# Six buffers instead of four for the two parts of every weight tile, and a 512-byte descriptor region

## The chip, the core and the metric

The kernel runs on one core of a Trainium2 chip. The metric is the device time of one execution in microseconds, the median of three runs. The engines are named as in the profile: PE multiplies matrices (PEld is its loading of weights), DVE, ACT and POOL work element by element, and SP only issues DMA transfers. Each engine takes its instructions strictly in the order in which the program gives them.

## The reference

For 256 tokens of width 1024 the reference computes a first block of two layers (pooling, an attention over chosen keys, a memory attention, three gated branches), a second block (a gated delta rule run over the tokens from both ends, a short convolution, two gated branches), and a gated MLP. All of it is float32. What matters here is the second block and the shape that all products with weights share:

```python
# every projection, shortened
proj = h @ w            # h: 256 x 1024, w: 1024 x (multiples of 256), float32

# second block, shortened: per head, from both ends of the sequence
S_t = exp(g_t) * S_{t-1} + beta_t * k_t (v_t - k_t S_{t-1} exp(g_t))^T
o_t = q_t S_t
y   = gate_dn * (norm(o) * silu(z)) @ w_branch_dn + gate_sc * conv(...) @ w_branch_sc
out = x + y @ w_out
```

## The kernel before, in words

**A product with weights.** PE multiplies in a float32 format of reduced precision, so an operand is split in a high part H and a low part L = value − H, and a product is the sum of three: xH·wH, xL·wH and xH·wL. The activations (names xH and xL) are split once. A weight matrix comes in blocks of 256 columns; a block with 1024 rows is two tiles of 128 partitions x 4 x 256 (512 KB each). For each tile SP issues the load (load(), L92 to L95, name raw, five buffers), ACT writes the high part (L107, name wH, four buffers), and DVE subtracts (L110, name wL, four buffers); in stretches where pool_l is 3, every third of these subtractions is POOL's. A *unit* of work for PE is one block: 2 halves of 128 columns x 8 row tiles x 3 products = 48 matmuls (mm3(), L123, from unit() or unit2(); units() at L151 runs two blocks side by side, with a part of the rows first). Four buffers hold the tiles of two units, six those of three.

**The second block.** After the first block's last product, x is scaled and split (L186), its squares are summed (L622, L625), PE adds them over the partitions (L631, name st), ACT takes the root (name sd), and DVE the reciprocal (L635, name St). Every result of q, k, v, z, the gates and the convolution is multiplied by St (for instance L672), so it is the first thing that all of DVE's later work in the block needs. The small product for the two gates of the delta rule (name ba, 48 columns) stands around it.

**The side chain.** delta() (L835 to L963) is a generator. Between units, pump() runs it on by a few steps, so its instructions are strewn among the units of q, k, v, z, the convolution (w_sc, w_branch_sc) and the gates (w_gate). It makes decay matrices (E, L899), inverts 32x32 blocks on DVE (inverse_blocks(), tm at L828, Tb at L830), copies the result transposed (L943, name Lb), sends both through memory (L946, to sT), and reads them back in three layouts (load_inverse(), L998 Tn, L1000 TBX, L1003 TT), all of it on SP's queue, between the weight loads. meta_state() (L967 to L986) makes the state after 16 leading tokens (names mtp, mkv at L976, mvn at L979, a copy on ACT at L980, ms at L984). whole_inverse() begins with the matmuls named x at L1016, which need Tn and TBX. Then half() and norm_gate() run for the heads 0 to 3 and 4 to 7: ks (L1082, L1084), vn (L1088, L1089), the states, the outputs o (L1119, L1123, copied at L1125), squares (L1134, osq) and their sums (L1136, osum), the norm (L1143) and the gate.

**What follows the chain.** drain() (L1228) empties the generator; its result is split (L1236, L1237, name oHL) and goes into the product with w_branch_dn (units(), L151, name mml), whose first part needs the heads 0 to 3 alone. Then come w_out_2 and the MLP.

**What sets the order.** The program is written in the order of the text, but the order in which each engine takes its instructions is chosen by a scheduler (`schedule_with_timeline_sim=True`, L1426), which plays the program through on a modelled timeline and also knows when a buffer comes free. With other numbers of buffers it chooses another order for all engines.

```python
for b in (1, 2):
    nc.sync.dma_start(out=TBX[32 * b:32 * b + 32, :, 0:32], in_=sT[0, b, 2 - b].rearrange("u i j -> i u j"))
...
TT, Tn, TBX = load_inverse(sT)
...
Sf0 = [meta_state(hf, mTt, dm) for hf in range(2)]
yield 2.0
for cst in whole_inverse(TT, Tn, TBX, LT64, LT32, nb64, nb32):
    yield cst
```

Of the kernel before, what the change touches and what calls it, by code (L numbers as in the profile page):

```python
# [8 lines left out]
F32R = mybir.dt.float32r  # L9
# [42 lines left out]
class _K:  # L52
# [44 lines left out]
    def weights(self, blk, kt, n):  # L97

        nc = self.nc
        parts = {}  # L100
        k0 = 0
        while k0 < kt:
            raw = self.ahead.pop(0) if self.ahead else self.load(blk, k0, min(4, kt - k0), n)
            m = raw.shape[1]
            H = self.wp.tile([128, 4, n], F32R, tag="wH", name="wH", bufs=4)[:, :m, :]
            L = self.wp.tile([128, 4, n], F32R, tag="wL", name="wL", bufs=4)[:, :m, :]
            nc.scalar.activation(H, raw, AF.Copy)  # L107
            self.n_l += 1
            e = nc.gpsimd if self.pool_l and self.n_l % self.pool_l == 0 else nc.vector
            e.tensor_tensor(L, raw, H.bitcast(F32), op=OP.subtract)  # L110
            for i in range(m):
                parts[k0 + i] = H, L, i
            k0 += m
        return [lambda k, a=a: parts[k][a][:, parts[k][2], :] for a in range(2)]
# [59 lines left out]
    def hl(self, pool, src, shape, tag, bufs=1):  # L174
        nc = self.nc
        H = pool.tile(shape, F32R, tag=tag + "H", name=tag + "H", bufs=bufs)
        L = pool.tile(shape, F32R, tag=tag + "L", name=tag + "L", bufs=bufs)
        nc.scalar.activation(H, src, AF.Copy)
        nc.vector.tensor_tensor(L, src, H.bitcast(F32), op=OP.subtract)
        return H, L  # L180

    def scaled_hl(self, H, L, x, g):

        nc = self.nc
        nc.scalar.activation(H, x, AF.Copy, scale=g)
        nc.vector.scalar_tensor_tensor(L, x, g, H.bitcast(F32), op0=OP.mult, op1=OP.subtract)  # L186
# [1244 lines left out]
```

## Time and profile before

| | |
|---|---|
| median of three runs | 1180.29 us (1178.58 to 1182.12) |
| profiled execution, its own time | 1179.4 us |
| its span | 1177.4 us |
| PE busy | 1114.1 us (95%), 9536 matmuls |
| DVE busy | 869.0 us (74%) |
| ACT busy | 586.7 us (50%) |
| POOL busy | 383.5 us (33%) |

The times that stand in front of a row count from the start of the span; the execution's own time is 2.0 us longer than the span. A busy time says how long an engine worked, not how long others waited for it. The views are read by stages: the first block (until about 570 us), the second block with its side chain (570 to 990), the MLP (990 to the end).

### The profile page before, as it was taken

The numbers are of one execution on the slowest core, as the hardware profiler recorded it, in microseconds if no ns is written. First come the engines' busy times: TensorE is split into PE (matmuls) and PEld (weight loads), VectorE is DVE, ScalarE is ACT, GpSimd is POOL, SyncE is SP. The second block draws the span as 40 slices with busy tenths as digits, with TensorE's granted clock in tenths as the row PEclk, the third lists the DMA queues.
The fourth block names the chain that finished last, engine by engine and source line by source line (L and its number), as shares of the span: only waits on it lengthen the run. The fifth ranks groups of instructions, "written<-read, shape, count | busy, mean of one in ns | idle before, by whom it ended". The sixth has DMA issues, their size and how long they took to land.

```text
span 1177.4 us, 23260 instructions
## 1 busy us (share of the span) xinstructions
PE 1114.1 (95%) x9536; PEld 1086.1 (92%) x9536; DVE 869.0 (74%) x1220; ACT 586.7 (50%) x883; POOL 383.5 (33%) x304
## 2 busy tenths in 40 slices
PE   6999999999999999999999878698899999999996
PEld 6999999999999999999998878697799999999996
DVE  8668897678665897977899899996547497555543
ACT  6344546446344454455675947242235645444442
POOL 8102310003100040100854668933011157534353
PEclk9999999999999999999999979898899999999999
DMA  7765453565655544455544525454432355556561
GB/s 262 268 211 170 156 173 123 180 192 182 196 192 182 179 133 136 147 177 180 186 169 144 181 82 144 134 175 105 148 126 94 134 187 180 200 172 199 180 193 40
DMA packets 68514, 194.63 MB, mean 165 GB/s; under 512 B 19504, under 2 KB 21816, under 8 KB 67896
## 3 DMA queue, kind: packets, MB, share of 16 engines
q1 hardware_dynamic: 66056, 188.72, 49.9%
q10 hardware_dynamic: 2352, 4.43, 1.1%
q8 instruction: 74, 1.21, 0.4%
q14 instruction: 32, 0.26, 0.1%
HBM read 189.39 MB, written 5.30 MB: 165 GB/s over the span
## 4 chain that ended last, share of the span: by engine, by line
PE 70%; DVE 17%; DMA 4%; issue 3%; ACT 2%; POOL 2%; SPq 1%; DVEq 0%; ACTq 0%; POOLq 0%
PE mm L123 49%; PE mml L151 8%; PE mmd L1302 5%; DVE wL L110 4%; DVE ac L685 2%; DVE Tb L830 1%; PE hp L372 1%; ACT wH L107 1%; DMA sT<-Lb 1%; DMA rows<-scr 1%; DVE tm L828 1%; DVE vf L685 1%; DVE kq L713 1%; PE mo L495 1%; PE vn L1088 1%
## 5 line engine op out<-in xcount | busy, mean ns | idle before, releaser
L110 DVE TENSOR_TENSOR wL<-raw,wH 128x1024 fp32r<-128x1024 f32 (+2 forms) x292 | 395.9, 1362 | 156.4 <-ACT wH L107 139.4
L107 ACT ACTIVATE wH<-raw 128x1024 fp32r<-128x1024 f32 (+3 forms) x347 | 347.0, 1034 | 302.4 <-PE mm L123 150.2
L123 PE MATMUL mm<-xH,wL 128*128 128x256 f32 (+3 forms) x1720 | 247.7, 284 | 11.2 <-DVE wL L110 11.2
L123 PE MATMUL mm<-xH,wH 128*128 128x256 f32 (+3 forms) x1720 | 249.0, 286 | 5.6 <-ACT ac L680 1.8
L123 PE MATMUL mm<-xL,wH 128*128 128x256 f32 (+3 forms) x1720 | 248.6, 285 | 0.0
L123 PEld LDWEIGHTS mm<-xH,wL 128*128 128x128 f32 (+1 forms) x1720 | 221.9, 190 | 13.5 <-DVE wL L110 12.3
L123 PEld LDWEIGHTS mm<-xH,wH 128*128 128x128 f32 (+1 forms) x1720 | 222.7, 190 | 9.5 <-ACT ac L680 2.0
L123 PEld LDWEIGHTS mm<-xL,wH 128*128 128x128 f32 (+1 forms) x1720 | 223.2, 191 | 2.8 <-issue 2.2
L110 POOL TENSOR_TENSOR wL<-raw,wH 128x1024 fp32r<-128x1024 f32 (+2 forms) x55 | 133.9, 2434 | 217.5 <-ACT wH L107 149.3
L397 POOL TENSOR_TENSOR bp<-bias,sc 128x1024 f32<-128x1024 f32 (+1 forms) x4 | 14.7, 3667 | 246.3 <-DVE sc L395 219.9
L123 PE MATMUL mm<-yH,wH 128*128 128x256 f32 x256 | 42.5, 286 | 4.9 <-ACT yH L1207 4.9
L123 PE MATMUL mm<-yL,wH 128*128 128x256 f32 x256 | 43.0, 286 | 4.3 <-DVE yL L1208 4.3
L123 PE MATMUL mm<-yH,wL 128*128 128x256 f32 x256 | 42.1, 285 | 0.0
L191 POOL TENSOR_TENSOR acc<-x 128x256 f32<-128x256 f32 x2 | 1.4, 722 | 123.6 <-DVE x L562 120.4
L123 PEld LDWEIGHTS mm<-yH,wH 128*128 128x128 f32 x256 | 35.6, 193 | 5.2 <-ACT yH L1207 5.1
L123 PEld LDWEIGHTS mm<-yL,wH 128*128 128x128 f32 x256 | 35.7, 193 | 5.1 <-DVE yL L1208 4.8
L123 PEld LDWEIGHTS mm<-yH,wL 128*128 128x128 f32 x256 | 35.5, 193 | 0.3 <-issue 0.3
L193 POOL TENSOR_TENSOR sq<-x 128x256 f32<-128x256 f32 x33 | 33.6, 1027 | 6.2 <-DVE x L562 5.5
L685 DVE SCALAR_TENSOR_TENSOR ac<-rc,cw,ac 128x271 f32<-128x271 f32 (+3 forms) x48 | 34.4, 753 | 0.0
L191 POOL TENSOR_TENSOR a<-x 128x256 f32<-128x256 f32 x3 | 2.8, 941 | 80.4 <-DVE x L562 74.8
L1302 PE MATMUL mmd<-aH,wH 128*128 128x256 f32 x176 | 28.6, 281 | 0.0
L1302 PE MATMUL mmd<-aH,wL 128*128 128x256 f32 x176 | 28.6, 281 | 0.0
(433 smaller groups left out, 1829.3 us busy)
## 6 DMA issues: line engine op xcount, KB each, us to landing
raw<-in_w_b SPq DMA_DIRECT2D x64, 512.0 KB, 4.1
raw<-in_w_a SPq DMA_DIRECT2D x55, 512.0 KB, 4.0
raw<-in_w_gu SPq DMA_DIRECT2D x44, 512.0 KB, 4.5
raw<-in_w_branch SPq DMA_DIRECT2D x24, 512.0 KB, 4.3
raw<-in_w_out SPq DMA_DIRECT2D x24, 512.0 KB, 3.8
raw<-in_w_qkv SPq DMA_DIRECT2D x24, 512.0 KB, 3.8
raw<-in_w_sc SPq DMA_DIRECT2D x24, 512.0 KB, 3.8
raw<-in_w_down SPq DMA_DIRECT2D x20, 512.0 KB, 4.4
```

Source lines behind the costliest of these rows:

```text
L107: nc.scalar.activation(H, raw, AF.Copy)
L110: e.tensor_tensor(L, raw, H.bitcast(F32), op=OP.subtract)
L123: self.last_mm = nc.tensor.matmul(ps, lt(a, kt), rt(b, kt), start=i == 0, stop=i == n - 1).ins
L151: self.last_mm = self.nc.tensor.matmul(ps[:, :N], w[a](k)[:, h * 128:h * 128 + 128], xs[b][:, k, :], start=k == 0 and (a, b) == (0, 0), st ...
L193: nc.gpsimd.tensor_tensor(tmp, x, x, op=OP.mult)
L372: nc.tensor.matmul(pp[p][:, j, :n], a[r, 2 * i + j, :], b(r, 2 * i + j), start=True, stop=True)
L397: nc.gpsimd.tensor_tensor(bp[:, :, :n], bias[:, :, off:], pen[:, None, :n].to_broadcast([128, 8, n]), op=OP.add)
L495: nc.tensor.matmul(ps[:, h, :], mv[:, mb, h * 128:h * 128 + 128], PT[:, mb, h, :], start=mb == 0, stop=mb == 1)
L685: V.scalar_tensor_tensor(ac[:, t0:t1], r[:, t0 + j - 2:t1 + j - 2], w[:, j:j + 1], ac[:, t0:t1], op0=OP.mult, op1=OP.add)
L713: (V if (i * 8 + h) % 3 else G).tensor_tensor(t, t, sl(h, i), op=OP.mult)
L828: eng.tensor_tensor(t, Lb[:, j + 1:, j:j + 1].to_broadcast([P, m, w]), Tb[:, j:j + 1, 0:w].to_broadcast([P, m, w]), op=OP.mult)
L1302: nc.tensor.matmul(pss[h][:, :S], w[a](k)[:, h * 128:h * 128 + 128], (aH, aL)[b][:, k0 + k, :], start=k0 + k == 0 and (a, b) == (0, 0), st ...
```

## The change

The two tile calls in weights() ask for six buffers instead of four. One buffer is 4 x 256 x 4 = 4096 bytes in each of the 128 partitions, so the four new ones take 16 KB of each partition. The call that makes the program sets the region that is kept in each partition for descriptors of transfers issued by software to 512 bytes, where it had 16384.

```diff
@@ -102,8 +102,8 @@
-            H = self.wp.tile([128, 4, n], F32R, tag="wH", name="wH", bufs=4)[:, :m, :]
-            L = self.wp.tile([128, 4, n], F32R, tag="wL", name="wL", bufs=4)[:, :m, :]
+            H = self.wp.tile([128, 4, n], F32R, tag="wH", name="wH", bufs=6)[:, :m, :]
+            L = self.wp.tile([128, 4, n], F32R, tag="wL", name="wL", bufs=6)[:, :m, :]
@@ -1419,7 +1419,7 @@
-    nc = bacc.Bacc("TRN2", target_bir_lowering=False, num_devices=1)
+    nc = bacc.Bacc("TRN2", target_bir_lowering=False, num_devices=1, dynamic_dma_scratch_size=512)
```

The counts of instructions stay as they are; the order on each engine moves. Three places are shown. The first is DVE at the start of the second block, around the reciprocal St. The number behind a name tells one tile of that name from another: wL_7093 is the second tile of the small product ba, wL_7336 belongs to the third unit after it. Before:

```order
L625 SCALAR_TENSOR_TENSOR a2_6848<-a1_6847,a2_6848 128x256
L110 TENSOR_TENSOR wL_7093<-raw_7090,wH_7092 128x192
L110 TENSOR_TENSOR wL_7166<-raw_7163,wH_7165 128x1024
L635 RECIPROCAL St_6845<-sd_7039 128x272
L672 TENSOR_TENSOR rc_7048<-mml_6937,St_6845 128x272
```

And now, from the same sum of squares to the same first use of St:

```order
L625 SCALAR_TENSOR_TENSOR a2_6848<-a1_6847,a2_6848 128x256
L110 TENSOR_TENSOR wL_7248<-raw_7245,wH_7247 128x1024
L110 TENSOR_TENSOR wL_7254<-raw_7251,wH_7253 128x1024
L110 TENSOR_TENSOR wL_7336<-raw_7333,wH_7335 128x1024
L635 RECIPROCAL St_6845<-sd_7039 128x272
L672 TENSOR_TENSOR rc_7048<-mml_6937,St_6845 128x272
```

Three subtractions stand where two stood, and they are those of later tiles; wL_7336 is the sixth tile behind wL_7093 and is written into the same buffer. On PE the last matmuls that read wL_7093 stand behind the sum st (name st2 here) from which St is made:

```order
L123 MATMUL mm2_7096<-xH_6811,wL_7087 48x272 x3
L631 MATMUL st2_7037<-a2_6848,ones_79 128x272
L201 MATMUL stat_7043<-a1_6847,ones_79 128x256
L123 MATMUL mm2_7096<-xH_6811,wL_7087 48x272
L123 MATMUL mm2_7096<-xH_6811,wL_7093 48x272 x4
```

So 19 of the 24 matmuls of ba now stand ahead of the sum, where all 24 stood behind it, and wL_7336 cannot be written before the last 4 have been done.

The second place is SP's queue around the transfers of the inverse through memory (sT). Before:

```order
L94 DMA raw<-in_w_sc 128x1024 x11
L94 DMA raw<-in_w_gate 128x1024 x2
L94 DMA raw<-in_w_branch_sc 128x1024
L946 DMA sT<-Tb 4x16x1024 x2
L946 DMA sT<-Lb 4x16x1024 x2
L998 DMA Tn<-sT 32x16x32 x2
L1000 DMA TBX<-sT 32x16x32
L998 DMA Tn<-sT 32x16x32 x2
L1000 DMA TBX<-sT 32x16x32
L1003 DMA TT<-sT 32x32x32 x4
L94 DMA raw<-in_w_gate 128x1024 x2
L94 DMA raw<-in_w_branch_sc 128x1024
```

Now:

```order
L94 DMA raw<-in_w_gate 128x1024 x2
L94 DMA raw<-in_w_branch_sc 128x1024
L94 DMA raw<-in_w_gate 128x1024 x2
L94 DMA raw<-in_w_branch_sc 128x1024
L94 DMA raw<-in_w_gate 128x1024
L946 DMA sT<-Tb 4x16x1024 x2
L946 DMA sT<-Lb 4x16x1024 x2
L998 DMA Tn<-sT 32x16x32 x2
L1000 DMA TBX<-sT 32x16x32
L94 DMA raw<-in_w_gate 128x1024
L998 DMA Tn<-sT 32x16x32 x2
L1000 DMA TBX<-sT 32x16x32
```

Four weight loads that stood behind the whole passage through sT stand ahead of it, and a fifth in its middle.

The third place is PE at the end of the side chain, from the last ks of the heads 4 to 7 on. Before:

```order
L1082 MATMUL ks<-Sfb,kq 128x128 x3
L123 MATMUL mm<-xL,wH 128x256 x2
L123 MATMUL mm<-xH,wL 128x256 x8
L123 MATMUL mm<-xH,wH 128x256 x8
L123 MATMUL mm<-xL,wH 128x256 x6
L1088 MATMUL vn<-vb,TT 128x128 x2
L1119 MATMUL o<-kq,Sf_9375 128x128
```

Now, to the first matmuls of w_branch_dn (mml):

```order
L1082 MATMUL ks<-Sfb,kq 128x128 x2
L1088 MATMUL vn<-vb,TT 128x128
L1119 MATMUL o<-kq,Sf_9375 128x128
...
L1123 MATMUL o<-At,vb 128x128 x2
L1136 MATMUL osum<-osq,ones 128x512
L151 MATMUL mml<-oHL,wH 128x256 x20
L1136 MATMUL osum<-osq,ones 128x512
L151 MATMUL mml<-oHL,wH 128x256 x10
L151 MATMUL mml<-oHL,wL 128x256 x4
```

The matmuls of the last gate units, 82 of which stood between this ks and the product with w_branch_dn, now stand ahead of the ks; none is left behind it.

## Rows read from the trace of the kernel before

**Rows 1.** The page: busy time of each engine with its share and its count, and the clock that PE was granted, one digit (tenths of full speed, 9 is 90% or more) for each fortieth of the span.

```profile
PE 1114.1 (95%) x9536; PEld 1086.1 (92%) x9536; DVE 869.0 (74%) x1220; ACT 586.7 (50%) x883; POOL 383.5 (33%) x304
...
PEclk9999999999999999999999979898899999999999
```

**Rows 2.** Busy time of each engine in stretches of the span. The columns are the stretch, its length, the busy time (and instructions) of PE, PEld, DVE, ACT and POOL, PE's granted clock, the share of the DMA engines and GB/s.

```profile
60.00:475.00 415.00, 414.60 (x3522) 404.94 (x3523) 312.64 (x469) 203.20 (x310) 53.17 (x51) 1.00 0.54 171
475.00:515.00 40.00, 38.46 (x339) 37.46 (x340) 34.18 (x48) 20.06 (x37) 4.67 (x1) 1.00 0.45 146
570.00:804.30 234.30, 202.60 (x1521) 195.12 (x1519) 221.55 (x331) 139.01 (x240) 150.33 (x128) 0.94 0.48 152
804.30:831.70 27.40, 19.70 (x130) 17.76 (x131) 12.37 (x20) 7.19 (x11) 4.52 (x4) 0.80 0.57 153
831.70:931.60 99.90, 99.59 (x1202) 96.75 (x1202) 56.51 (x91) 42.13 (x54) 13.38 (x6) 0.97 0.32 106
...
1020.00:1050.00 30.00, 30.00 (x257) 30.00 (x256) 16.55 (x16) 13.53 (x16) 13.09 (x7) 1.00 0.56 180
```

**Rows 3.** Waits over the whole span, by the waiting engine and line and the engine and line that ended the wait: us in total, how often, the longest.

```profile
ACT wH L107 <- PE mm L123: 150.2, 68, 5.2
...
PE mm L123 <- DVE wL L110: 11.2, 6, 5.6
...
PE mvn L979 <- DVE mkv L976: 4.7, 1, 4.7
```

**Rows 4.** The timeline around St. The columns, here and in the timelines below, are start, duration (of the whole group where a count stands at the end), engine, line, operation and shapes; in brackets the engine's idle time before it and what ended it.

```profile
583.79 0.70 PE L631 MATMUL st<-a,ones 128*128 128x272 f32 x2 [0.40 <-PE mml L151]
...
584.57 1.33 PE L123 MATMUL mm<-xH,wH 128*48 128x272 f32 x8
...
585.20 1.85 DVE L635 RECIPROCAL St<-sd 128x272 f32<-128x272 f32 x1 [0.36 <-ACT sd L89]
...
586.74 1.16 PE L123 MATMUL mm<-xH,wL 128*48 128x272 f32 x8
...
588.49 1.22 DVE L110 TENSOR_TENSOR wL<-raw,wH 128x1024 fp32r<-128x1024 f32 x1
```

**Rows 5.** The timeline from the end of the block inverse on DVE to the first matmul of whole_inverse().

```profile
804.27 1.03 DVE L943 COPY Lb<-Tb 128x1024 f32<-128x1024 f32 x1
...
807.55 0.41 DVE L1188 TENSOR_TENSOR cS<-mm,St 128x258 f32<-128x258 f32 x1
...
819.27 0.48 SPq L1000 DMA_DIRECT2D TBX<-sT  x1
...
823.22 0.98 SPq L94 DMA_DIRECT2D raw<-in_w_gate  x2
...
828.08 1.06 ACT L107 ACTIVATE wH<-raw 128x1024 fp32r<-128x1024 f32 x1 [8.01 <-DMA raw<-in_w_gate]
829.04 0.57 ACT L980 ACTIVATE mkv<-mvn 16x512 f32<-16x512 f32 x1
...
829.67 2.07 PE L984 MATMUL ms<-mkv 16*128 16x128 f32 x8 [5.46 <-ACT mkv L980]
...
831.67 0.26 PE L1016 MATMUL x<-Tn,LT 32*32 32x32 f32 x1
```

**Rows 6.** Transfers issued between 790 and 835 us: count, KB each, median us from issue to landing.

```profile
TBX<-sT SPq DMA_DIRECT2D x2, 64.0 KB, 7.1
```

**Rows 7.** The timeline at the end of the side chain.

```profile
913.32 1.13 DVE L1084 SCALAR_TENSOR_TENSOR vb<-ks,be,vb 128x128 f32<-128x128 f32 x4 [0.60 <-PE ks L1082]
...
923.59 0.61 PE L1123 MATMUL o<-At,vb 128*128 128x128 f32 x4
...
928.66 1.02 PE L1136 MATMUL osum<-osq,ones 128*128 128x512 f32 x2
...
930.42 1.06 ACT L107 ACTIVATE wH<-raw 128x1024 fp32r<-128x1024 f32 x1
...
937.23 1.13 ACT L1236 ACTIVATE oHL<-vf 128x512 fp32r<-128x512 f32 x2
```

**Rows 8.** The timeline of DVE and POOL at one place of the block inverse, and all 31 instructions of DVE's line there (ns: least, median and longest; the first and the last start; the most frequent shapes).

```profile
749.93 5.05 DVE L830 TENSOR_TENSOR Tb<-Tb,tm 128x112 f32<-128x112 f32 x1
...
750.22 2.33 POOL L110 TENSOR_TENSOR wL<-raw,wH 128x1024 fp32r<-128x1024 f32 x1
...
752.52 2.33 POOL L929 TENSOR_TENSOR qb<-kq,Gb 128x1024 f32<-128x1024 f32 x1
...
L830 DVE TENSOR_TENSOR Tb<-Tb,tm x31: 193/390/5054, 743.8 to 804.0; 128x31 f32<-128x31 f32 x2, 128x60 f32<-128x60 f32 x2, 128x87 f32<-128x87 f32 x2, 128x112 f32<-128x112 f32 x2
```

**Rows 9.** The timeline of PE near the end of the first block.

```profile
495.36 0.74 PE L123 MATMUL mm<-xH,wL 128*128 128x256 f32 x4 [0.73 <-DVE wL L110]
...
502.21 0.74 PE L123 MATMUL mm<-xH,wH 128*128 128x256 f32 x4 [0.81 <-ACT wH L107]
```

**Rows 10.** The page: the DMA queues with their kind, packets, MB and share of the 16 engines' span.

```profile
q1 hardware_dynamic: 66056, 188.72, 49.9%
q10 hardware_dynamic: 2352, 4.43, 1.1%
q8 instruction: 74, 1.21, 0.4%
q14 instruction: 32, 0.26, 0.1%
```

## The prediction

> **What bounds the kernel now.** First the page's busy times: PE 95%, DVE 74%, ACT 50% [rows 1]; the reader sees one engine that is nearly always busy, so deeper buffers can win at most what PE still waits. Then the windows, to see where PE is not busy [rows 2]. From 60 to 475 us PE works 414.60 of 415.00 us, and nothing that DVE or ACT do earlier can help. From 570 to 804.3 PE works 202.60 of 234.30, and DVE 221.55: this stage belongs to DVE (12.75 us idle). From 804.3 to 831.7 neither is full (19.70 and 12.37 of 27.40): a stage of waits. From 831.7 to 931.6 PE is full again (99.59 of 99.90). Then the waits [rows 3]: ACT waits 150.2 us in 68 places for PE to free a buffer of wH, while PE waits for DVE's wL only 11.2 us, in 6 places. So most of the time the four buffers are full because PE is the slow one; more buffers let DVE and ACT run further ahead, which pays only where PE later finds work that it had to wait for. The longest single wait of PE that hangs on this is in [rows 5]: ms at 829.67 waited 5.46 us for a copy on ACT, and that copy stood behind a wH conversion that waited 8.01 us for its weight load.
>
> **The change part by part.** Instruction counts stay, so all of it is order and waits. The sum is made against the profiled execution (1179.4, span 1177.4), 0.9 us under the median of 1180.29.
>
> *St.* St starts at 585.20 [rows 4]. In the new order the third subtraction ahead of it, wL_7336, goes into the buffer of wL_7093, which PE frees with ba's last 4 matmuls. A matmul of ba takes 1.16/8 = 0.145 us [rows 4]. Without the old order PE would start ba at 583.79 − 0.40 = 583.39; 19 matmuls take it to 586.15, st and stat some 0.7 more (by the same row), 5 matmuls 0.7: free at 587.5. On DVE the subtraction (1.22 us [rows 4]) then ends at 588.7, and St starts 3.3 us later than before (588.5; I take a little off because POOL may do a share of DVE's earlier work). Behind the waiting subtraction on DVE stands St and so everything that needs St. Below zero it can't go, since three more subtractions of 1.22 us stand ahead of St than before; above, it is 3 × 1.22 = 3.7. So 0 to 3.7, taken 3.3, near the upper end, because DVE is the bound of this stage.
>
> *DVE from St to Lb.* 35 subtractions stand there before and after. Two more small operations fall into it, 0.41 us each [rows 5]: +0.8. POOL gets one more subtraction (2.33 us [rows 8]) ahead of Lb; POOL and DVE disturb each other (rival 2), for which I take half of it, +1.2, between 0 and 4.7 (two of them). Lb moves from 804.27 to 804.27 + 3.3 + 0.8 + 1.2 = 809.6.
>
> *From Lb to x (L1016).* Before, 831.67 − 804.27 = 27.4 us, of which the last part was ms, waiting for ACT, waiting for a load of w_gate that was issued at 823.22 only, since it stood behind the passage through sT on SP's in-order queue [rows 5]. Four of those loads stand ahead of the passage now, so this wait of 5.46 goes. What is late next is TBX: issued at 819.27, landing 7.1 us later [rows 5, 6], at 826.4, which is 22.1 us behind Lb. So x starts between 22.1 and 27.4 us behind Lb; the upper end is the case where the five loads of 512 KB moved in front take from the transfers what the wait gives back. I take 22.1, the chain that is left: 809.6 + 22.1 = 831.7, the same as before. The gain in this stage and the loss in front of it cancel.
>
> *Work pulled ahead of x.* By the new order 5788 matmuls of weights and of the chain stand ahead of the first x on PE where 5759 stood, 29 more. From x on PE is full, so they come off what follows: 29 × 30.00/257 = 29 × 0.117 [rows 2] = −3.4. If PE had to wait inside the stage for these as well, it is 0; if x moves, it moves with it.
>
> *The end of the chain.* Before, 82 matmuls of the gates stood between the last ks and the product with w_branch_dn and filled PE's waits; now nothing but the first part of w_branch_dn does (the 64 matmuls that read heads 0 to 3 alone). The chain from ks to the split result: 1.13 for the vb on DVE, about 7.1 for vn and o on PE (the o at 923.59 ends the work that in the new order is packed), 0.6 for the copy, 0.62 for the squares, and from osum to oHL 937.23 − 928.66 = 8.57 less the 1.06 of a wH conversion that stood in it [rows 7] = 7.5, then 0.6 to the end of the first half of oHL: 17.6 us. PE's work beside it is 7.1 of vn and o, 1.0 of osum [rows 7], 64 × 0.117 = 7.5: 15.6. What is left open is 2.0, so +2.0 (from 0, if the wH conversions in between move off the chain and the first 64 are slowed, to 3.2 with the conversion back in it). The 82 matmuls are not lost: they were done earlier, where PE would have had to do something else.
>
> *The first block.* Near its end PE waits 0.73 for wL and 0.81 for wH [rows 9], in a window with 1.54 us open [rows 2]. Deeper buffers should remove one of the two: −0.8 (0 to −1.5).
>
> *The region.* All queues are fed by hardware or by instructions [rows 10], none by software descriptors; a smaller region costs 0.
>
> Sum: 0 at x, −3.4, +2.0, −0.8 = −2.2. 1179.4 − 2.2 = 1177.2, and with the 0.9 between execution and median 1178.1.
>
> **The rivals.** *Rival 1, DVE has room: faster.* The 12.75 us that DVE idles between 570 and 804.3 [rows 2] take up the late St, the two operations and POOL's share, and Lb stays at 804.27; x then starts at 826.4, 5.3 us earlier: 1178.1 − 5.3 = 1172.8. For it: DVE's idle time is not one wait that is fixed. Against it: the idle time is spread, and the chain of the inverse on DVE has only short steps with nothing between. The furthest end of this case is that all waits of PE for wL go, 11.2 us [rows 3]: 1180.29 − 11.2 = 1169.1. The Trainium skill's "Perfetto Trace Analysis" (Identifying the Most-Contended Engine) says that the same gap repeating on the engine that should be saturated can mean that there is no room in SBUF or PSUM for the next tile. By that rule the added buffers should close the gaps, and the time would be at that end; the trace agrees only in part, since six waits make up the 11.2 us and ACT's 150.2 point the other way.
>
> *Rival 2, DVE and POOL collide more often: slower.* The place is the side chain on DVE between St and Lb. At 749.93 a Tb takes 5.05 us where the median of the line is 0.39; in the same time POOL runs two operations of 2.33 us [rows 8]. So one collision costs DVE 2.3 us (one POOL operation) to 4.7 (5.05 − 0.39). The new order puts other, and more, POOL subtractions beside DVE's. Three more such meetings of 2.33 make 7.0, and Lb and x move by as much: 1178.1 + 7.0 = 1185.1. It decides from about 5.7 us on (1183.8 − 1178.1), that is from three short or two long meetings. For it: this stage is DVE's, and POOL works 150.33 of 234.30 us in it [rows 2]. Against it: the number of POOL's operations hardly changes, and new meetings replace old ones. The Trainium skill's "SBUF — State Buffer" (SBUF: two separate sides) says that the shared port pair is an exclusive lock, held for a whole instruction by whichever of a DVE operation with two SBUF inputs and a POOL operation starts first. The trace agrees: 5.05 is two POOL operations of 2.33 and the 0.39.
>
> *Rival 3, nothing that counts moves.* The buffers are full because PE is slow (150.2 us of ACT's waits); the order of the side chain changes, but the sums of it cancel to zero: 1180.3.
>
> PE's clock is a cost that I put at nothing: it was granted 0.94, 0.80 and 0.97 of full speed in the three windows from 570 to 931.6 [rows 2], so it stood for part of them at the lower of its two levels (1.2 instead of 2.4 GHz). If the stage from 804.3 on ran at full clock, that is at most 27.4 × 0.20 = 5.5 us; if it fell as low in one more stretch of that length, as much is lost. This widens the range on both sides and is in both rivals' chances.
>
> **How the numbers follow.** Within 0.3% of 1180.29 (1176.7 to 1183.8) is about what a measurement of this kernel can't tell from no change. My forecast has a chance of 0.42, with its own range of 1174.5 to 1182 from the bounds of its terms; of that 0.10 lies under 1176.7, 0.30 inside and 0.02 above. Rival 1 has 0.24, all faster. Rival 2 has 0.22, all slower. Rival 3 has 0.12: 0.10 inside and 0.01 on each side. Together faster 0.35, same 0.40, slower 0.25. The range goes from 1169 (the furthest end of rival 1) to 1187 (rival 2 with about four meetings: 1178.1 + 9.3).
>
> **What would show it.** St should start near 588.5 instead of 585.20, in the row where DVE's wL before it waits for PE's mm; Lb near 809.6. The wait of ACT for in_w_gate (8.01) and that of PE at ms (5.46) should be gone, and PE should wait before x (L1016), released by the transfer to TBX or Tn. Behind the last ks PE should show waits of 2 us in all, at vn or at mml for oHL. Rival 1 would show Lb at 804 to 805; rival 2 rows of L828, L830 or L685 on DVE of 2 to 7 us beside POOL's subtractions, more of them than before. The prediction is wrong if PE gets waits in 60 to 475 us, if the window from 831.7 on is no longer full, or if the stage between Lb and x stays at 27 us with another load in the place of w_gate's.

## The result and the profile after

The changed kernel takes 1187.99 us (median of 4 runs, 1185.71 to 1189.34) against 1180.99 of the kernel before, run beside it (4 runs): a ratio of 1.0063, 95% interval 1.0042 to 1.0083. A second job gave 1187.87 and 1.0067 (1.0044 to 1.0091). It is slower by 7 us, clear of noise; 1178.1 was forecast, and the range ended at 1187.

The profiled execution took 1188.02 us, its span is 1186.2. The windows with the borders of [rows 2], and one for the first 75 us:

```profile
60.00:475.00 415.00, 412.28 (x3491) 403.14 (x3490) 311.23 (x465) 201.70 (x309) 53.00 (x51) 1.00 0.53 172
475.00:515.00 40.00, 39.21 (x352) 38.11 (x351) 36.96 (x52) 22.28 (x39) 4.67 (x1) 1.00 0.45 145
...
570.00:804.30 234.30, 206.00 (x1542) 199.33 (x1540) 217.45 (x317) 138.01 (x240) 153.18 (x130) 0.95 0.47 152
804.30:831.70 27.40, 23.21 (x168) 21.50 (x168) 22.41 (x42) 11.09 (x16) 10.78 (x6) 0.88 0.50 150
831.70:931.60 99.90, 92.86 (x1128) 90.50 (x1128) 53.59 (x89) 35.46 (x44) 14.97 (x6) 0.95 0.40 127
931.60:990.00 58.40, 53.12 (x435) 51.22 (x435) 39.58 (x55) 30.42 (x45) 24.72 (x16) 0.97 0.41 136
...
0.00:75.00 75.00, 62.45 (x472) 59.84 (x473) 52.55 (x60) 35.08 (x51) 28.78 (x38) 0.95 0.76 256
```

The reader sees PE gain where it waited for DVE (206.00 of 234.30 after 202.60, 23.21 of 27.40 after 19.70) and lose where it was full: 92.86 of 99.90 after 99.59. And in this profile it loses at the very beginning, where nobody looked: the same window of the kernel before was

```profile
0.00:75.00 75.00, 64.40 (x515) 61.95 (x516) 53.32 (x61) 34.67 (x50) 28.80 (x38) 1.00 0.75 257
```

that is, 43 matmuls more in the same time, at a granted clock of 1.00 instead of 0.95. Where the loss comes in by stages is read from the starts of five rows on each timeline: the first xL of the second block, St, the copy Lb (L943), the last oHL (L1236), and the span.

| | first xL | St | Lb | last oHL | span |
|---|---|---|---|---|---|
| before | 561.28 | 585.20 | 804.27 | 937.74 | 1177.4 |
| after | 564.77 | 594.15 | 814.06 | 947.60 | 1186.2 |
| after, second profile | 566.10 | 595.48 | 815.69 | 949.00 | 1187.7 |

The first block hands on 3.5 us (second profile: 4.8); from the first xL to St 5.5 more are lost (29.38 for 23.92); from St to Lb it is the same length (219.91 and 219.07), from Lb to the last oHL too (133.5 and 133.5), and behind it the rest is a little shorter. One profile of each kernel is compared here, and single profiles scatter: see the end of the next part.

**The beginning.** ACT's timeline of the kernel after, 41 to 58 us. scr, rows and bias are three transfers of a small table through memory, issued by ACT itself:

```profile
41.67 1.06 ACT L107 ACTIVATE wH<-raw 128x1024 fp32r<-128x1024 f32 x1 [3.15 <-PE mm L123]
42.13 0.55 ACTq L245 DMA_DIRECT2D scr<-btmp  x1
42.64 1.05 ACT L107 ACTIVATE wH<-raw 128x1024 fp32r<-128x1024 f32 x1
45.79 0.55 ACTq L248 DMA_DIRECT2D rows<-scr  x1
...
57.84 2.01 ACT L107 ACTIVATE wH<-raw 128x1024 fp32r<-128x1024 f32 x2 [8.67 <-DMA rows<-scr]
```

and of the kernel before:

```profile
38.59 0.55 ACTq L245 DMA_DIRECT2D scr<-btmp  x1
40.17 2.01 ACT L107 ACTIVATE wH<-raw 128x1024 fp32r<-128x1024 f32 x2 [3.20 <-PE mm L123]
43.39 0.56 ACTq L248 DMA_DIRECT2D rows<-scr  x1
...
54.54 2.01 ACT L107 ACTIVATE wH<-raw 128x1024 fp32r<-128x1024 f32 x2 [6.91 <-DMA rows<-scr]
```

The order says the same: scr stood ahead of two wH conversions and stands behind them now, and the first of these waits 3.15 us for PE to free a buffer. scr is issued 3.5 us later, but that wait is not all of it. The table that scr sends is copied by DVE (L243, name btmp) from a product of PE. DVE's timeline before:

```profile
38.02 0.54 DVE L243 COPY btmp<-vec 8x384 f32<-8x384 f32 x1
```

and after, with one more subtraction ahead of the copy:

```profile
39.09 1.21 DVE L110 TENSOR_TENSOR wL<-raw,wH 128x1024 fp32r<-128x1024 f32 x1
40.23 0.54 DVE L243 COPY btmp<-vec 8x384 f32<-8x384 f32 x1
```

So 2.2 of the 3.5 us are there before ACT is reached: PE starts the product 1.55 us later (38.23 for 36.68), and DVE's subtraction makes some 0.7. Only 1.3 are ACT's conversions. ACT then goes on 3.3 us later (57.84 for 54.54). At the end of that chain PE waits, 2.59 us (4.67 in the second profile) where it waited 0.83, as its timelines before and after show:

```profile
60.30 0.61 PE L212 MATMUL tok<-ident,Smem 128*128 128x1 f32 x4 [0.83 <-DVE Smem L204]
...
63.61 0.61 PE L212 MATMUL tok<-ident,Smem 128*128 128x1 f32 x4 [2.59 <-DVE Smem L204]
```

How much of this comes from the order, and how much from one execution? The runs of the next section answer it, since many of them keep one order or the other through the first block. With the order of the changed kernel there are five profiles: PE waits 2.52 to 4.67 us at L212 in four of them and not at all in six_block1, and the first xL starts at 561.2 to 566.1 us, 564.2 on average. With four buffers for the first 24 tiles at least, and no other order up to the 75th us, there are thirteen: the wait is 0 to 1.93, and the first xL starts at 558.4 to 565.9, 561.8 on average. So the order costs some 2.4 us here, and one profile can be off by more than that.

**St**, the timeline that answers to [rows 4]:

```profile
588.20 0.43 DVE L625 SCALAR_TENSOR_TENSOR a<-a,a 128x256 f32<-128x256 f32 x1
...
588.54 5.69 DVE L110 TENSOR_TENSOR wL<-raw,wH 128x1024 fp32r<-128x1024 f32 x3
590.39 2.75 POOL L110 TENSOR_TENSOR wL<-raw,wH 128x1024 fp32r<-128x1024 f32 x1 [3.12 <-PE mm L123]
...
590.70 0.47 ACT L89 ACTIVATE sd<-st,e 128x256 f32<-128x256 f32 x1
594.15 1.84 DVE L635 RECIPROCAL St<-sd 128x272 f32<-128x272 f32 x1
...
596.52 1.37 PE L123 MATMUL mm<-xH,wH 128*128 128x272 f32 x8 [2.78 <-DVE rc L672]
```

The root sd is ready at 591.17; the three subtractions of later tiles stand ahead of St until 594.15. They take 5.69 us, not 3 x 1.22 = 3.66. The first two take 1.22 each; the third, beside one of POOL, takes 3.39 (DVE's timeline from 590.9 us on):

```profile
590.84 3.39 DVE L110 TENSOR_TENSOR wL<-raw,wH 128x1024 fp32r<-128x1024 f32 x1
```

POOL's ends at 593.14; from there the third needs another 1.09. PE then waits 2.78 for the first use of St.

**Behind Lb**, the timeline that answers to [rows 5, 7]:

```profile
814.06 1.12 DVE L943 COPY Lb<-Tb 128x1024 f32<-128x1024 f32 x1
...
829.70 0.49 SPq L1000 DMA_DIRECT2D TBX<-sT  x1
830.23 4.36 SPq L1003 DMA_DIRECT2D TT<-sT  x4
...
833.77 0.31 PE L1016 MATMUL x<-Tn,LT 32*32 32x32 f32 x2 [2.12 <-DMA Tn<-sT]
...
846.50 0.18 PE L1024 MATMUL t<-TBX,TT 32*32 32x32 f32 x1 [3.97 <-issue]
927.65 0.49 PE L1088 MATMUL vn<-vb,TT 128*128 128x128 f32 x2 [0.44 <-DVE vb L1084]
931.73 0.71 PE L1123 MATMUL o<-At,vb 128*128 128x128 f32 x4 [0.69 <-ACT vb L1089]
937.21 2.55 PE L151 MATMUL mml<-oHL,wH 128*128 128x256 f32 x20 [0.34 <-ACT oHL L1236]
946.28 1.21 PE L151 MATMUL mml<-oHL,wH 128*128 128x256 f32 x8 [1.57 <-ACT wH L107]
947.75 2.42 PE L151 MATMUL mml<-oHL,wH 128*128 128x256 f32 x19 [0.26 <-ACT oHL L1236]
966.41 1.86 PE L151 MATMUL mml<-mHL,wH 128*128 128x256 f32 x7 [2.98 <-ACT mHL L185]
```

The waits of 8.01 on ACT and 5.46 on PE are gone; in their place PE waits 2.12 for Tn, 3.97 in the middle of the matmuls at L1024 and L1027 (names t and t10t), 3.30 in five places at the end of the chain, and 2.98 ahead of w_out_2. For the 3.97 the profile names no releaser ("issue"). These matmuls read TT, but they had been running since 840.89, and the small packets that fill TT had ended by 839. What does end shortly before is a packet of 16 KB on the queue of kind "instruction" (q8 in [rows 10]), at 845.15, 1.35 us before PE goes on. In sixteen of the twenty profiles PE has such a gap near this place, 0.81 to 4.92 us long, and each time such a packet ended 1.26 to 1.60 us before. That PE waits there for its instructions is likely, not shown. Nor does the gap tell the slower kernel from the others: both_four, which takes the time of before, has it too (PE's timeline of both_four).

```profile
837.11 0.23 PE L1030 MATMUL t10t<-TT,TBX 32*32 32x32 f32 x5 [3.69 <-issue]
```

### The profile page after: what moved, and what is told of

Read it like the earlier page. It is cut to its first block, busy times and chain, and to the rows that moved or that the text cites. A ratio compares the mean times of both kernels' runs of the same rounds, so it can differ in the third digit from the quotient of the medians.

```text
span 1186.2 us, 23294 instructions
## 1 busy us (share of the span) xinstructions
PE 1119.0 (94%) x9536; PEld 1092.4 (92%) x9536; DVE 862.9 (73%) x1220; ACT 584.6 (49%) x883; POOL 383.9 (32%) x304
## 4 chain that ended last, share of the span: by engine, by line
PE 75%; DVE 14%; DMA 4%; issue 3%; ACT 2%; SPq 1%; POOL 0%; DVEq 0%; ACTq 0%; POOLq 0%
PE mm L123 51%; PE mml L151 10%; PE mmd L1302 5%; DVE wL L110 3%; DVE ac L685 2%; DVE tm L828 2%; DVE Tb L830 1%; PE hp L372 1%; DMA rows<-scr 1%; PE kkq L906 1%; PE mo L495 1%; PE vn L1088 1%; DMA raw<-in_w_a 1%; PE o L1119 1%; ACT wH L107 1%
## 5 line engine op out<-in xcount | busy, mean ns | idle before, releaser
L110 DVE TENSOR_TENSOR wL<-raw,wH 128x1024 fp32r<-128x1024 f32 (+2 forms) x292 | 402.4, 1386 | 154.3 <-ACT wH L107 151.8
L123 PE MATMUL mm<-xH,wH 128*128 128x256 f32 (+3 forms) x1720 | 251.5, 288 | 23.5 <-DVE cS L1188 10.6
L123 PEld LDWEIGHTS mm<-xL,wH 128*128 128x128 f32 (+1 forms) x1720 | 225.7, 193 | 1.9 <-issue 1.3
L110 POOL TENSOR_TENSOR wL<-raw,wH 128x1024 fp32r<-128x1024 f32 (+2 forms) x55 | 130.5, 2372 | 188.3 <-ACT wH L107 146.5
L685 DVE SCALAR_TENSOR_TENSOR ac<-rc,cw,ac 128x271 f32<-128x271 f32 (+3 forms) x48 | 30.5, 669 | 0.0
L1302 PE MATMUL mmd<-aL,wH 128*128 128x256 f32 x176 | 28.6, 281 | 0.0
```

The costliest lines, as they stand in the source:

```text
L123: self.last_mm = nc.tensor.matmul(ps, lt(a, kt), rt(b, kt), start=i == 0, stop=i == n - 1).ins
L685: V.scalar_tensor_tensor(ac[:, t0:t1], r[:, t0 + j - 2:t1 + j - 2], w[:, j:j + 1], ac[:, t0:t1], op0=OP.mult, op1=OP.add)
L1302: nc.tensor.matmul(pss[h][:, :S], w[a](k)[:, h * 128:h * 128 + 128], (aH, aL)[b][:, k0 + k, :], start=k0 + k == 0 and (a, b) == (0, 0), st ...
```

## The experiments

The number of buffers can be set by stage. A ring of six is four buffers of one tag and two of another; where `wide` is off, only the four are used. In the traces a stage with `wide` on has the order of the changed kernel (six_block1 and front_four, the first block), and one with it off, beside the small region, that of the kernel before (six_front, the first block; four_lb_late, up to its extra copies). So the region moves nothing there; alone it was not run. The edit, shortened:

```diff
-            H = self.wp.tile([128, 4, n], F32R, tag="wH", name="wH", bufs=6)[:, :m, :]
+            j = self.n_w % 6 >= 4 if self.wide else 0
+            self.n_w += 1
+            H = self.wp.tile([128, 4, n], F32R, tag=("wH", "wH2")[j], name="wH", bufs=(4, 2)[j])[:, :m, :]
...
```

**Six buffers in one stage alone.** K.wide is on in the first block; from the start of the second block to the end of q and k (the front); in the loop of z, v, convolution and gates; or behind drain().

> Six buffers in the first block alone, four from the second block on; the order from the second block on is that of before. Theory A (the 4.8 us that PE falls behind in the first 75 us of the changed kernel stay to the end): 1184 to 1186. Theory C (the loss is made by six buffers in the loop of the side chain, which use up the gate units before the chain ends): the lag of some 3 us at 570 us is swallowed in the stage that waits for DVE, 1179 to 1182. Theory B (St late) says as C, since the order around St is the old one.

> Six buffers from the start of the second block to the end of q and k, four elsewhere. Three subtractions stand ahead of St as in the changed kernel, and 83 gate matmuls behind the last ks as before. Theory B (St and with it the whole side chain come late, and that is the loss): St at 590 to 592, 1185 to 1188. Theory C: the late chain finds the gate units behind it and PE goes on working, 1179 to 1182. Theory A: 1180.

> Six buffers only in the loop of z, v, convolution and gates, beside which the side chain runs; the order around St is the old one; 29 gate matmuls stand behind the last ks where 82 did, and six weight loads stand ahead of or within the passage through sT as in the changed kernel. Theory C: PE waits at TT or x and at the end of the chain, 1184 to 1188. Theories A and B: 1179 to 1181.

> Six buffers only behind the side chain (w_branch_dn, w_out_2, MLP). All theories: 1179 to 1182; if the longer wait at w_out_2 (2.98 us with a fall of the clock behind it, where before it was 1.63) comes from here, 1182 to 1183.

Measured, as ratios to the kernel before: first block 1.0012 (0.9995 to 1.0029), front 1.0049 (1.0029 to 1.0069), loop 1.0013 (0.9998 to 1.0028), tail 1.0026 (1.0008 to 1.0043). In us the medians are 1181.68, 1185.22, 1181.09 and 1183.59. Theory A, the beginning, misses its 1184 to 1186; in six_block1's profile scr is as late as in the changed kernel (42.87), but PE doesn't wait at L212. Theory C, the loop, falls, though the loop's profile has the gap at t10t, 4.92 us. Theory B is right for the front, which costs most, 5.8 us by the ratio. The tail is outside all forecasts. In the front, St starts at 591.57, 30.9 us behind the first xL. Here sd itself is late, and the reader sees on ACT why: it stands behind two conversions for later tiles, the first of which waits for its load (timeline of six_front).

```profile
586.93 2.25 ACT L110 ACTIVATE wH<-raw 128x1024 fp32r<-128x1024 f32 x2 [2.25 <-DMA raw<-in_w_qkv]
589.07 0.26 ACT L90 ACTIVATE sd<-st,eps 128x16 f32<-128x16 f32 x1
```

**St put first by force.** The subtractions for ba and the next units are queued behind St on DVE, and ba behind st on PE (order only, no wait). The edit, shortened:

```diff
-            e.tensor_tensor(L, raw, H.bitcast(F32), op=OP.subtract)
+            with self.tc.issue_after(self.st):     # where St has been written in the text
+                e.tensor_tensor(L, raw, H.bitcast(F32), op=OP.subtract)
...
-    pba = unit2(A["w_ba"], 48, 0)[0]
+    with K.tc.issue_after(K.st2):
+        pba = unit2(A["w_ba"], 48, 0)[0]
```

> Six buffers from the start of the second block to the end of q and k, as in six_front, but the subtractions for ba and the next units are queued behind St on DVE, and ba behind the sum st on PE: one subtraction is left ahead of St instead of three. Theory B (the late St makes the chain late, and that is the loss of 5.8 us): St at 584 to 586, the copy Lb at 804 to 809 instead of 814.0, 1179 to 1181. Rival (the six buffers lose elsewhere in that stretch, by DVE and POOL meeting more often, and St is only where it shows first): St early, Lb still at 812 or later, 1184 to 1187.

> The changed kernel with the same edit: no subtraction ahead of St, ba behind st; 250 weight loads ahead of the passage through sT and no gate matmul behind the last ks, as in the changed kernel. Theory B: St at 585 to 588, Lb at 805 to 809, and some 5 us of the 7.5 come back: 1181 to 1184. Rival: 1186 to 1189.

> Four buffers, with the same edit: the 1.5 us of the two subtractions go from in front of St. Theory B: St at 583 to 584, 1178 to 1180. Rival: 1179 to 1181, no difference.

> As four_st_first, but the reciprocal St is computed four times in a row: three more of 1.85 us, so St is ready 5.5 us later with four buffers and 83 gate matmuls behind the last ks. Theory B with its full price (a late St is paid one to one, unless the work that PE has left behind x covers it): 1183 to 1186. If the price of a late St hangs on the deeper buffers only: 1178 to 1181.

All four missed: 1.0082 (1.0054 to 1.0110), 1.0106 (1.0078 to 1.0134), 1.0104 (1.0076 to 1.0132) and 1.0082 (1.0049 to 1.0115). With four buffers St comes hardly earlier behind the first xL (23.8 us for 23.9), the forced order alone costs 1%, and three more reciprocals in front of it cost nothing on top. So theory B in its plain form, a late St is paid one to one, falls; and a rule that holds preparations back altogether does more harm than the few that stand in the way.

**A late Lb, and the two halves of the change.**

```diff
-        V.tensor_copy(Lb, Tb.rearrange("p a b -> p b a"))
+        for _ in range(6):
+            V.tensor_copy(Lb, Tb.rearrange("p a b -> p b a"))
```

> The kernel before with the copy Lb at L943 done seven times instead of once: six more of 1.03 us on DVE, 6.2 us, at the end of the block inverse and nowhere else. Theory D (in the profiles so far the time goes with the start of Lb: 804 us with spans of 1177 to 1180, 809 with 1179, 814 with 1182 to 1186, 817 to 821 with 1189 to 1193, so a late chain is paid nearly one to one): the last copy at 811 to 814, 1184 to 1187. Theory C' (four buffers leave 49 gate matmuls behind the last ks, and PE does these while it waits, so a late Lb costs nothing unless the buffers are deep): 1179 to 1182.

> Six buffers for wH, four for wL, so ACT may run ahead by two tiles more and DVE may not. Two more subtractions stand ahead of St than before (188 for 186), one more ahead of Lb (222 for 221; the changed kernel has 224), and 6 gate matmuls behind the last ks. Theory D: Lb at 805 to 809, 1180 to 1184. Theory E (no gate matmuls are left at the end, and that is the loss): 1184 to 1187.

> Six buffers for wL, four for wH. A subtraction needs its wH, so DVE gains no room to run ahead; 186 subtractions ahead of St and 221 ahead of Lb as before, 52 gate matmuls behind the last ks. Theory D: Lb at 803 to 805, 1179 to 1182. Theory E: 1180 to 1182.

> The changed kernel once more, unchanged, for a second profile: how much of what the first showed comes again. Theory D: Lb at 810 to 815 again. If the 4.8 us that PE lost in its first 75 us are the luck of one execution (a fall of the clock at 30.9 us behind the same waits as before, a transfer that landed 1.8 us later), they are 0 to 2 here and Lb is at 810 to 811; if they come from the order, they are 4 to 5 again. Time in both cases 1185 to 1189.

four_lb_late, which makes six copies of Lb instead of one (the text on record speaks of seven): 1.0011 (0.9992 to 1.0030). The last copy starts at 818.01, 13.7 us later than before (the first at 807.73), and the time stays. Theory D, that the time goes with Lb, falls. But that PE fills the delay with gate matmuls, theory C', isn't what the profile shows: x is not late. It starts at 829.89 and goes on at 831.39, where it stood at 831.67 before, since Tn and TBX are issued later but ACT no longer waits for a load of w_gate (PE's timeline of four_lb_late):

```profile
831.39 0.31 PE L1017 MATMUL x<-Tn,LT 32*32 32x32 f32 x2 [1.25 <-DMA Tn<-sT]
```

What a late x costs with four buffers stays open. six_high_only: 1.0150 (1.0109 to 1.0191), twice the loss of the whole change and outside both forecasts, with one subtraction more ahead of Lb; this is not explained by any theory here beyond what its profile shows: St starts 30.5 us behind the first xL, sd again behind conversions that wait for loads, and PE then waits 3.17 and 5.05 us in the front. six_low_only: 1.0024 (1.0005 to 1.0043), just outside the forecast of no change. six_again repeats the result and, with 4.67 us at L212, the loss at the beginning.

**Parts taken out of the whole.** Since parts alone don't say what they cost together, the ring was narrowed in the changed kernel: for the first 24 tiles, in the front, in both, and in both and behind the chain. The edits, shortened:

```diff
+            j = self.n_w % 6 >= 4 if self.wide and self.n_w >= 24 else 0
...
+            K.wide = False      # front_four, both_four: from the start of the second block
...
+    K.wide = True               # to the end of q and k
```

> The changed kernel, but the first 24 weight tiles use four of the six buffers: on ACT the transfer of the table to memory (name scr, L245) stands ahead of two wH conversions again, where the changed kernel has it behind them. Everything else stands as in the changed kernel (189 subtractions ahead of St, 224 ahead of Lb, 250 loads ahead of the passage through sT, no gate matmul behind the last ks). Theory F (the table comes 2 to 3 us later in the changed kernel, the first wait of PE with the fall of the clock behind it is 3 to 5 us, and this stays to the end): the wait of PE at L212 near 61 us under 1.5 us, 1183 to 1185. Rival (swallowed by the stage that waits for DVE): 1187 to 1189.

> The changed kernel, but four of the six buffers from the start of the second block to the end of q and k: 186 subtractions ahead of St as before, still 224 ahead of Lb, 13 gate matmuls behind the last ks, the table late as in the changed kernel. Theory G (that stretch costs what six_front showed, 5.8 us): 1181 to 1184. Rival (the loss of the stretch is only seen where the loop behind it has four buffers): 1186 to 1189.

> Both together. If F and G hold and add: 1179 to 1181, the time before. If only one of them holds: 1182 to 1185. If neither: 1186 to 1189.

> As both_four, and four of the six buffers also behind the side chain (w_branch_dn, w_out_2, MLP). If the 3.1 us that six_tail showed come from there: 2 to 4 us less than both_four. If not: the same as both_four within 1.5 us.

| | ratio | 95% interval | first xL | St | Lb | last oHL | span |
|---|---|---|---|---|---|---|---|
| changed kernel | 1.0063, 1.0067 | 1.0042 to 1.0083, 1.0044 to 1.0091 | 564.77 | 594.15 | 814.06 | 947.60 | 1186.2 |
| start_four | 1.0033 | 1.0019 to 1.0046 | 563.45 | 592.83 | 812.97 | 946.28 | 1185.0 |
| front_four | 1.0025 | 1.0002 to 1.0048 | 564.25 | 587.76 | 814.60 | 947.41 | 1186.0 |
| both_four | 0.9968 | 0.9949 to 0.9987 | 558.39 | 581.91 | 805.04 | 936.41 | 1173.7 |
| both_four, second job | 1.0002 | 0.9992 to 1.0013 | 559.65 | 583.17 | 807.65 | 939.11 | 1179.0 |

Each of the two parts gives back about half (0.3 and 0.4%), and both together all of it: the results are on the side of F and G, and they add. The medians (1185.62, 1184.10 and, together, 1177.88 and 1180.80) are off the ranges on record by up to 1.1 us, but for the last. Together is measured in two jobs, each part by itself in one. In start_four scr is issued at 39.23 again, but PE still waits 1.88 us at L212, over the bound of F, and its first xL (563.45) stands where the scatter of this order has its late end. The profiled executions of start_four (1186.90; median 1185.62) and front_four (1187.80; median 1184.10) are the second slowest and the slowest of their runs, so their rows stand on the high side; that of both_four (1175.60) is on the low side. three_four gives 0.9996 (0.9978 to 1.0015), 2.6 us slower than both_four in the same job instead of 2 to 4 faster: the 3.1 us of six_tail are not part of the loss. Six buffers in the loop and behind it are therefore harmless in this order.

**The order around St, or q behind it.**

> As both_four, but four of the six buffers only from the start of the second block to the end of k (the units around St), and six again for q: 186 subtractions and two of later tiles ahead of St as before, no gate matmul behind the last ks. Theory H (the loss of that stretch is the late St): as both_four, 1176 to 1180. Rival (it is the deeper buffers of q behind St): as start_four, 1184 to 1187.

> both_four once more, with more rounds, on the chip of st_four. If it is faster than the kernel before, as its first interval says: 0.2 to 0.5% below it. If that was the luck of one chip: within 0.15% of it.

st_four: 1.0041 (1.0026 to 1.0056); both_four_again: 1.0002 (0.9992 to 1.0013). By the text on record the rival wins. But the premise failed: DVE has its old order, and St is late all the same, 586.97, 26.7 us behind the first xL where both_four has 23.5. Its ACT shows the third form of the same thing, a conversion for q that waits for its load, with sd behind it (timeline of st_four):

```profile
585.36 1.06 ACT L110 ACTIVATE wH<-raw 128x1024 fp32r<-128x1024 f32 x1 [2.17 <-DMA raw<-in_w_qkv]
586.32 0.26 ACT L90 ACTIVATE sd<-st,eps 128x16 f32<-128x16 f32 x1
```

So the run doesn't part the two. And both_four is not a faster kernel: its gain of 0.3% didn't come again, on the same chip, so it was the luck of one job and not of a chip. No version was found that beats the kernel before.

## Why the prediction was wrong

**What was shown.** The loss sits in two stretches, the first 24 tiles and the front of the second block: with four buffers in both it is gone (two jobs), with four in one of them about half of it is (one job each). That is where it is, by experiment; the mechanism in each is read from rows. In both, with two buffers more, the scheduler puts preparations for later tiles ahead of a single instruction that much else waits for, in a queue that goes in order: the table's copy behind a wL on DVE and scr behind two wH on ACT, St behind three wL on DVE, sd behind wH on ACT. **What stays open** is whether the delay of St is itself what the front loses. In the orders that the scheduler chose freely, St 26.7 to 30.9 us behind the first xL goes with a loss (six_front, st_four, six_high_only, start_four and the changed kernel), and 23.5 to 23.9 with a ratio of at most 1.0026 (both_four, three_four, six_loop, six_tail, six_block1, front_four, six_low_only, four_lb_late); with a forced order (four_st_first, four_st_late) the time didn't follow St.

**By the steps of the forecast.** The sum said −2.2 for the profiled execution; the span grew by 8.8. The 11.0 us between them are 4.3 in the first block, 2.2 at St, −1.2 from St to Lb, 6.8 from Lb to the last oHL and −1.1 behind it. So two steps failed, and one term was too small.

*The first block, −0.8: a step that failed.* The step expected to remove one of the two waits of [rows 9], and it did (39.21 of 40.00 us busy after 38.46, +0.75). But the step looked only at PE's waits near 500 us and not at what the new order does to DVE and ACT in the first 60, where a table's copy and its transfer were moved behind preparations. The first block came out 3.5 us longer, 4.3 us off this term (by the averages over profiles above, some 2.4 longer). A sign that the prediction had named came with it: PE waits between 60 and 475 us (412.28 of 415.00 busy after 414.60).

*St, +3.3: mis-sized.* The three subtractions and the later st were as described; the delay from the first xL on is 5.5 us, above the bound of 3.7. The bound counted 1.22 for a subtraction, and the third, beside POOL's, took 3.39. Without these 2.2 us the delay would be 3.3, as forecast.

*From St to Lb, +2.0.* Measured +0.8 (219.91 for 219.07). DVE has three operations more (318 for 315), POOL's extra share cost nothing that shows.

*From Lb to x, 22.1 with x at 831.7.* The first x started at 831.29, a hit by luck: Lb came 4.5 us later than forecast, and x 17.2 us behind Lb, below the lower bound. TBX issued 15.6 us behind Lb (before, 15.0), and the last of Tn and TBX let PE go on at 833.77, 4.1 us after TBX's issue, not 7.1. The stall of w_gate's load did go.

*29 matmuls, −3.4: the other step that failed.* PE did run ahead, by these 29. But the step rests on "from x on PE is full", and it is not (92.86 of 99.90 in that window). From the first x to the last oHL the changed kernel takes 116.3 us, before 106.1, and the sum had 104.7: what was gained ahead of x went into waits behind it, 2.12 at x, 3.97 without a named releaser and the 3.30 of the next term, and into a lower clock. From Lb to the last oHL the forecast gained 6.7 us (5.3 + 3.4 − 2.0), and nothing was gained. In both profiles of both_four, which has the six buffers there but neither loss, this stage takes 131.4 us: 2.1 less than before, not 6.7.

*The end of the chain, +2.0.* Five waits make 3.30, a little over the upper bound of 3.2: 1.04 at vn and at mml for oHL, the places named, 1.57 for a wH conversion, the case of that bound, and 0.69 at an o.

*The clock, 0.* It was granted 0.95 and 0.97 in the two windows from 831.7 to 990, before 0.97 and 1.00: some 0.02 x 99.9 + 0.03 x 58.4 = 3.8 us lost. In the two windows from 570 to 831.7 it was higher than before, 0.95 for 0.94 and 0.88 for 0.80: 0.01 x 234.3 + 0.08 x 27.4 = 4.5 gained. From 570 us on this nearly cancels, so zero was right for the sum and not for its parts. What is left is the first 75 us, 0.95 for 1.00: 3.8 us, as much as the whole shift of the first block in this pair of profiles. Not all of it is the order's: three_four has 0.95 there too, and both_four, with the same order, 1.00.

**The rivals.** Rival 1 (DVE has room) was wrong: DVE's room took up nothing of the late St. The sentence of the Trainium skill's "Perfetto Trace Analysis" that it cites stands there under Optimization Strategy. Rival 2 had the sign, but not the mechanism. The window of the kernel after from St to Lb:

```profile
594.15:814.06 219.91, 189.38 (x1391) 183.19 (x1392) 207.33 (x318) 126.25 (x221) 136.79 (x108) 0.93 0.45 142
```

From St to Lb DVE is busy 207.33 us with 318 instructions; before, it was 209.97 with 315 in 219.07 us. If it met POOL more often, it would be busy longer. And the sign of rival 2, more rows of 2 to 7 us at L828, L830 or L685, isn't there: eight with 22.2 us in all (the longest 4.52, a tm), before nine with 24.6 (the longest the 5.05 of [rows 8]). One meeting did count, that of the third subtraction ahead of St, 2.2 us, at a place that rival 2 didn't name; there POOL's operation started first (590.39 for 590.84). In [rows 8] the Tb starts 0.29 us ahead of POOL's, so these rows agree with rival 2's price but don't show that the one that starts first is the one that is served. Rival 3 was wrong too: the order counts.

## What to carry to other kernels

More buffers for operands that an engine prepares ahead don't only remove waits: in queues that go in order, the preparations move in front of other things, and a look at the order should ask of each engine which single instruction, that much waits for, now stands behind a preparation that itself waits for a buffer or a load. The places with a small gain (PE's rare waits) are soon counted; the places where nothing was wrong before, as the first 60 us here, need the same look. And it is worth measuring a part's cost both ways, put in alone and taken out of the whole: alone, the first block cost 0.12% with an interval that includes zero, taken out its first 24 tiles gave back 0.3%. These intervals overlap, so which is nearer stays open.

## What the runs showed that was not expected

The clock can fall behind the same waits in one execution and not in another. In the kernel before PE waited 1.32, 0.92 and 0.55 us from 27.66 on, and eight matmuls then took 1.07 us; in the changed kernel the waits were 1.31, 0.92 and 0.54, and eight matmuls took 1.92, at the lower of the two levels (1.2 instead of 2.4 GHz; timeline of the kernel after).

```profile
30.41 0.83 PE L123 MATMUL mm<-xH,wL 128*128 128x256 f32 x4 [0.54 <-DVE wL L110]
31.04 1.92 PE L123 MATMUL mm<-xH,wH 128*128 128x256 f32 x8
```

Two runs with the same order up to there, both_four and st_four, show it with waits that are equal to within 0.01 us (PE's timelines of the two):

```profile
30.22 0.74 PE L126 MATMUL mm<-xH,wL 128*128 128x256 f32 x4 [0.78 <-DVE wL L113]
30.79 1.07 PE L126 MATMUL mm<-xH,wH 128*128 128x256 f32 x8
...
30.20 0.74 PE L126 MATMUL mm<-xH,wL 128*128 128x256 f32 x4 [0.78 <-DVE wL L113]
30.77 1.87 PE L126 MATMUL mm<-xH,wH 128*128 128x256 f32 x8
```

The clock falls near 30 us in fifteen of the twenty profiles, with four buffers and with six; the kernel before was profiled in one of the five where it doesn't.

And an interval from one job can be too narrow: the same kernel gave 0.9968 (up to 0.9987) in one and 1.0002 (from 0.9992) in another. Differences of 0.3% here need two jobs, and those of start_four and front_four have one.
